# Seven-product blocks with turned signs: weight sums of a tile by accumulating DMA, sums of the second weights in one shared tile, and one borrowed weight slot

## The chip, the core and the metric

The kernel runs on one core of a Trainium2 chip. A core has TensorE (PE: matrix products; PEld is its weight load), VectorE (DVE), ScalarE (ACT), GpSimd (POOL) and SyncE (SP), which here only issues DMAs; sixteen DMA engines move data between HBM, the on-chip memory SBUF and back. Every engine works through its own list of instructions in order, and engines wait for each other through semaphores. Products land in PSUM, from where DVE and ACT take them. The metric is the device time of one launch in microseconds (us); less is better.

## The reference, cut to what matters

One step of a two-layer streaming encoder in float32: 1024 new frames and 64 sample frames, so 1088 columns of width 1024. Layer 0 is a Mamba-2 mixer, layer 1 is banded attention; each layer ends with the same feed-forward block, and the change touches only that block:

```python
def swiglu(u, w_in, w_out):
    g, up = jnp.split(u @ w_in, 2, axis=-1)
    return (jax.nn.silu(g) * up) @ w_out

xp = xp + rmsnorm(swiglu(rmsnorm(xp, nw[2]), ffn_w_in[layer], ffn_w_out[layer]), nw[3])
```

`w_in` is 1024 x 5632 (a gate half and an "up" half of 2816 = 22 tiles of 128 columns), `w_out` is 2816 x 1024.

## The kernel before, in words

**Precision.** A float32 operand is split into a high part in the 32-bit format that PE takes (`h`, made by a CAST on ACT, L354) and the rest (`lo`, a subtraction, L355, on DVE, or on POOL for one operand). A product is three matmuls: high x high, high x low, low x high (L1338, L1339, L1340).

**Seven products.** Weights and activations are cut in 2 x 2 blocks and multiplied with the seven products and fifteen sums of Strassen and Winograd. For pair `t` of weight tiles, `r0` is the gate tile, blocks b11 and b21, and `r1` is the up tile, blocks b12 and b22; each block is 128 x 512. The operands of the seven products (table `PRODS`) are `r0` (P1, P2), `ta` (P6, P7), `tb` (P5, P4) and `b22` (P3). Before, `Weights.pair` makes them so: POOL subtracts b22 - b12 (L302) and b12 - b11 (L303) into the tiles `tt`, DVE adds b11 (L320) and subtracts the result from b21 (L321), ACT and DVE split `r0`, `ta` and `tb` (three 128 x 1024 splits a pair), ACT and POOL split `b22` (128 x 512).

**Slots.** Split weights live in rings: `hl` of 3 slots (high and low, 1024 wide), `half` of 2 slots for `b22`, `raw` of 2 slots for what a DMA has just brought, `tt` of 2. A slot comes free after its last product: `W.put()` stands behind P2 (`r0`), P7 (`ta`), P4 (`tb`) and P3 (`half`) in the order P1, P6, P2, P7, P5, P4, P3.

**Stages of the feed-forward block,** in both layers. (1) Six pairs of tiles are multiplied plainly for the first column half (`plain_pairs`, lines "mmx"). (2) One pair, `t` = 6, is multiplied with seven products first for column block b = 0 (256 columns), then for b = 1 (288 columns); here called the first pair. (3) Fifteen pairs with both blocks in turn, so that a product's weights serve 544 columns: the shared pairs. (4) The six pairs of stage 1 again, for b = 1 alone, since b = 0 has them: the single pairs. A weight that serves 288 columns here costs the same splits. (5) The second weights `w_out`, seven products again (lines "po"), with the hidden activations read back from HBM (`hscr`).

**Gates.** The results of P1 to P7 are added up by DVE out of PSUM (L1353 to L1370, eight instructions of 288 or 256 columns a pair and block), with a SiLU on ACT (L1356, L1366) and two products on POOL (L1367 `u`, L1371 `c`). DVE then makes the sums of the hidden activations for stage 5 (L1469, L1477), which read `c` and `u` from POOL. In stage 3 DVE also makes the sums of the second weights (L1414), four instructions a job, 20 jobs a layer, with two tiles of their own (`r` 288 wide, `z` 272 wide); they are stored to HBM (`wsum`).

**What sets the order.** The kernel is recorded by a planner: `Stream` advances a clock by the columns that PE works through, side tasks come due on it, and a scheduler places the recorded instructions by priorities (`high_priority`) and dependencies, with a few ties given by hand (`add_manual_dep`, `behind`). PE's order is as written.

Of the kernel before, what the change touches and what calls it, by code (L numbers as in the profile page):

```python
# [43 lines left out]
RB_WAIT = 4.8  # L44
CHW = ((13.1, 8.8, 18.0), (7.5, 6.0, 20.5)), ((9.0, 5.2, 15.0), (10.5, 8.0, 21.0))
# [24 lines left out]
LENT = 3  # L70
SUM_P = 2.0
# [161 lines left out]

class Weights:
# [4 lines left out]
    def __init__(self, nc, raw, hl, half, tt):  # L239
        self.nc, self.raw, self.hl, self.half, self.tt = nc, raw, hl, half, tt  # L240
# [5 lines left out]
        self.raws, self.lent = [raw], None  # L246

        self.hx, self.used = Ring(None, "hx", 0, hl.shape, hl.dtype), []

    def plan(self, *items):  # L250
        for it in items:
# [3 lines left out]
            self.sq.append(it)  # L255

    def load(self):
# [4 lines left out]
        self.loaded = self.nc.sync.dma_start(r[:, :it.get("n", 1024)], it["src"][len(it["raw"])])  # L262
# [6 lines left out]
    def advance(self):  # L269
        moved = True  # L270
        while moved:
            moved = False
            while self.lq and any(r.free() for r in self.raws):
                self.load()
# [4 lines left out]
    def room(self):  # L279
        return self.hl.free() or self.hx.free()  # L280
# [13 lines left out]
    def pair(self, it):  # L294
        r0, r1 = it["raw"]
        b11, b21, b12, b22 = r0[:, :512], r0[:, 512:], r1[:, :512], r1[:, 512:]
        if "T" not in it:
            if not self.tt.free(2):
# [3 lines left out]
            g(ta[:, 512:], b22, b12, op=ALU.subtract)  # L302
            g(tb[:, :512], b12, b11, op=ALU.subtract)  # L303
            return True
        ta, tb = it["T"]
# [4 lines left out]
        if "r0" not in it:  # L310
            if not self.hl.free():
                return False
            self.part(it, "r0", self.hl, r0)
            self.ready.append(it)

            return False
        if "sums" not in it:
            v = self.nc.vector.tensor_tensor
            with self.tc.high_priority(self.pri):
                v(ta[:, :512], ta[:, 512:], b11, op=ALU.add)  # L320
                v(tb[:, 512:], b21, ta[:, :512], op=ALU.subtract)  # L321
            it["of"][0].put()
            it["sums"] = True
            return True
        for key, src in (("ta", ta), ("tb", tb)):
            if key not in it:
                if not self.hl.free():
# [1927 lines left out]
```

## Time and profile before

| | |
|---|---|
| median of 3 runs | 2914.21 us (2914.08 to 2914.99) |
| the profiled execution | 2919.82 us |
| its span, first to last instruction | 2918.0 us, so 1.8 us lie around it |
| mean granted TensorE clock | 0.995 |
| busy PE / DVE / ACT / POOL | 98% / 75% / 47% / 25% |
| layer 0, stages 2, 3, 4, 5 begin at | 917.8, 943.7, 1256.3, 1330.9 us |
| layer 1, the same | 2260.1, 2284.5, 2597.1, 2671.4 us |

The starts are those of the first matmul of a kind in the timeline. "Idle" in the profile's views is time before an instruction in which its engine did nothing, with the instruction that ended the wait behind an arrow. A view of windows gives each engine's busy time in a stretch, with the number of its instructions in brackets, the granted clock, the share of time that the 16 DMA engines were busy, and GB/s.

### The profile page before, as it was taken

To read this page: it belongs to the slowest core of one execution; us is meant where nothing else is said; L and a number is where in the kernel's file an instruction comes from. 1 tells how busy PE (TensorE), PEld (TensorE's weight loads), DVE (VectorE), ACT (ScalarE), POOL (GpSimd) and SP (SyncE) were. 2 spreads that over 40 slices of the span, in tenths; PEclk is the share of its full clock that TensorE was granted. 3 is DMA by queue.
4 is the path that set the end of the run, shared out by engine and by line. 5 is a ranking of instruction groups with operands and counts; after the bars stand their busy time and mean duration, and the time that the engine had idled before them with its cause. 6 is when DMAs were issued, how large, how long until landed. Compare 5 with 4: busy or idle time off the path is not lost. (4 is left out here: it accounts for less than half of the span.)

```text
span 2918.0 us, 58367 instructions
## 1 busy us (share of the span) xinstructions
PE 2852.8 (98%) x22094; PEld 2805.7 (96%) x22094; DVE 2191.3 (75%) x4994; ACT 1383.5 (47%) x2564; POOL 726.5 (25%) x900
## 2 busy tenths in 40 slices
PE   8999999999999999999998999999999999999999
PEld 8999999999999999999997899999999999999998
DVE  7987888885768667785569778777778876776567
ACT  6654546454444222244445556556565322334443
POOL 1333333331122343441021000000041334343011
PEclk9999999999999999999999999999999999999999
DMA  4423333244565556446564222222377455555656
GB/s 139 126 99 101 107 101 103 96 125 144 177 183 157 168 175 194 160 159 209 183 194 156 61 80 79 74 64 82 96 220 214 152 180 175 178 176 169 203 189 196
DMA packets 271530, 426.23 MB, mean 146 GB/s; under 512 B 25360, under 2 KB 202736, under 8 KB 271248
## 3 DMA queue, kind: packets, MB, share of 16 engines
q1 hardware_dynamic: 268016, 411.94, 44.4%
q0 software_dynamic: 3232, 10.56, 2.0%
q8 instruction: 174, 2.85, 0.4%
q14 instruction: 108, 0.88, 0.1%
HBM read 313.74 MB, written 104.19 MB: 143 GB/s over the span
## 5 line engine op out<-in xcount | busy, mean ns | idle before, releaser
L480 PE MATMUL mm<-r,hl 128*128 128x384 f32 (+2 forms) x1704 | 569.0, 334 | 6.1 <-DVE vt L1872 3.9
L481 PE MATMUL mm<-r,hl 128*128 128x384 f32 (+2 forms) x1704 | 551.4, 324 | 2.4 <-DVE r L1586 2.4
L482 PE MATMUL mm<-r,hl 128*128 128x384 f32 (+2 forms) x1704 | 551.1, 323 | 2.1 <-DMA hl<-in_w_in_dram 1.4
L1339 PE MATMUL px<-r,hl 128*128 128x288 f32 (+1 forms) x1184 | 348.1, 294 | 0.0
L480 PEld LDWEIGHTS mm<-r,hl 128*128 128x128 f32 x1704 | 323.4, 190 | 8.4 <-DVE vt L1872 4.2
L481 PEld LDWEIGHTS mm<-r,hl 128*128 128x128 f32 x1704 | 323.2, 190 | 3.3 <-DVE r L1586 3.0
L482 PEld LDWEIGHTS mm<-r,hl 128*128 128x128 f32 x1704 | 322.0, 189 | 2.8 <-DMA hl<-in_w_in_dram 1.7
L1340 PE MATMUL px<-r,hl 128*128 128x288 f32 x1056 | 312.7, 296 | 3.2 <-DVE hl L355 3.1
L1338 PE MATMUL px<-r,hl 128*128 128x288 f32 x1056 | 311.3, 295 | 2.8 <-DVE u L1353 2.1
L355 DVE TENSOR_TENSOR hl<-raw,hl 128x1024 fp32r<-128x1024 f32 (+2 forms) x172 | 193.7, 1127 | 99.1 <-ACT hl L354 98.8
L1712 PE MATMUL po<-r,hl 128*128 128x288 f32 (+1 forms) x856 | 246.9, 288 | 0.1
L1710 PE MATMUL po<-r,hl 128*128 128x288 f32 (+1 forms) x856 | 246.9, 288 | 0.0
L1711 PE MATMUL po<-r,hl 128*128 128x288 f32 (+1 forms) x856 | 246.9, 288 | 0.0
L1339 PEld LDWEIGHTS px<-r,hl 128*128 128x128 f32 x1184 | 223.0, 188 | 0.0
L354 ACT CAST hl<-raw 128x1024 fp32r<-128x1024 f32 (+2 forms) x172 | 166.5, 968 | 114.0 <-PE po L1712 34.3
L1340 PE MATMUL px<-rx,hl 128*128 128x256 f32 x768 | 215.0, 280 | 3.7 <-DVE hl L355 3.6
L1338 PE MATMUL px<-rx,hl 128*128 128x256 f32 x768 | 214.5, 279 | 1.5 <-ACT hl L354 1.5
L1340 PEld LDWEIGHTS px<-r,hl 128*128 128x128 f32 x1056 | 199.4, 189 | 4.6 <-DVE hl L355 4.6
L1338 PEld LDWEIGHTS px<-r,hl 128*128 128x128 f32 x1056 | 199.5, 189 | 3.7 <-DVE u L1353 2.5
L1339 PE MATMUL px<-rx,hl 128*128 128x256 f32 x640 | 178.9, 280 | 0.0
L1710 PEld LDWEIGHTS po<-r,hl 128*128 128x128 f32 x856 | 161.5, 189 | 0.0
L1712 PEld LDWEIGHTS po<-r,hl 128*128 128x128 f32 x856 | 160.9, 188 | 0.3 <-DVE hl L355 0.3
(385 smaller groups left out, 8152.2 us busy)
## 6 DMA issues: line engine op xcount, KB each, us to landing
raw<-in_w_f_dram SPq DMA_DIRECT2D x104, 512.0 KB, 4.2
raw<-in_w_in_dram SPq DMA_DIRECT2D x40, 512.0 KB, 3.9
MT<-ascr SPq DMA_DIRECT2D x48, 384.0 KB, 4.4
r<-hscr SPq DMA_DIRECT2D x58, 288.0 KB, 4.2
raw<-in_w_so_dram SPq DMA_DIRECT2D x32, 512.0 KB, 3.8
r<-in_w_f_dram SPq DMA_DIRECT2D x48, 288.0 KB, 3.4
wsum<-r SPq DMA_DIRECT2D x24, 576.0 KB, 3.4
r<-hscr SPq DMA_DIRECT2D x40, 256.0 KB, 4.2
```

The source lines that it names most:

```text
L354: self.nc.scalar.copy(h, v)
L355: (eng or self.eng or self.nc.vector).tensor_tensor(lo, v, h, op=ALU.subtract)
L480: PE.matmul(ps[:, :n], h_, xh, start=(first and i == 0), stop=False)
L481: PE.matmul(ps[:, :n], h_, xl, start=False, stop=False)
L482: PE.matmul(ps[:, :n], l_, xh, start=False, stop=(last and i == nk - 1))
L1338: PE.matmul(ps, wh, ah[:, k, :], start=(k == 0), stop=False)
L1339: PE.matmul(ps, wh, al[:, k, :], start=False, stop=False)
L1340: PE.matmul(ps, wl, ah[:, k, :], start=False, stop=(k == 3))
L1710: PE.matmul(ps, wh, xh, start=(k0 > 0 and i == ks[0]), stop=False)
L1711: PE.matmul(ps, wh, xl, start=False, stop=False)
L1712: PE.matmul(ps, wl, xh, start=False, stop=(k0 == 0 and i == ks[-1]))
```

## The change

Four things, all in the feed-forward block.

- **Signs turned, sums by DMA.** The four sums of a pair are taken with plus signs only; the activations' sums and the gates take the minus signs, one for one (a subtraction for an addition). SP loads b11 and b12 side by side into a tile of `tt` (a 2 x 512 pattern), and POOL issues an accumulating DMA that adds b12 and b22 to it from HBM: T = (b11 + b12, b12 + b22). DVE makes S = (T2 + b11, S1 + b21) into a tile of its own, `t2`. T and S are split as `ta` and `tb` were. `r1` is now only b22, and `b22` of every pair is split by two ACT instructions and an accumulating DMA on POOL, as four of the 44 were before. POOL's subtractions L302, L303 and L355 are gone. The first of two planner times, `ACC_W` = 5.0, stands between the load of T and its accumulation.
- **Products in another order:** P1, P6, P2, P7, P4, P5, P3; `s2` serves P6 and P4, `s1` P7 and P5. So `s2`'s slot comes free after P4 (the fifth product), `s1`'s after P5 (the sixth).
- **One job at a time for the sums of the second weights,** in one shared tile of the ring `R`, at any product whose gate result DVE has taken, with the planner time `SUM_W` = 4.5 from load to sums and from store to the next load. The tile pool `z` is gone, `t2` takes its place.
- **A borrowed slot:** in stage 4 (`HPC[0]` = 1; none in stage 5, `HPC[1]` = 0) a pair of tiles of the ring `RX` serves as a fourth slot beside `hl`.

```diff
+HPC = 1, 0
+class Pairs:          # two tiles of a ring, as high and low part of one slot
+    def free(self):
+        return self.live < self.cap and self.ring.free(2)
...
 class Weights:
     def advance(self):
         moved = True
         while moved:
             moved = False
+            while self.tq and self.tt.free():
+                it = self.tq.pop(0)
+                it["T"] = self.tt.get()
+                self.loaded = self.nc.sync.dma_start(it["T"].rearrange("p (e k) -> p e k", e=2), it["two"][0])
...
+                self.aq.append((self.clock() + ACC_W, it))
+            while self.aq and self.aq[0][0] <= self.clock() and 'two' in self.sq[0]:
+                it = self.aq.pop(0)[1]
+                x = self.nc.gpsimd.dma_start(it["T"], it["two"][1], accum_op=ALU.add)
...
     def pair(self, it):
         r0, r1 = it["raw"]
-            ta, tb = it["T"] = self.tt.get(), self.tt.get()
-            g = self.nc.gpsimd.tensor_tensor
-            g(ta[:, 512:], b22, b12, op=ALU.subtract)
-            g(tb[:, :512], b12, b11, op=ALU.subtract)
...
         if "b22" not in it and self.half.free():
-            self.part(it, "b22", self.half, b22, self.nc.gpsimd, it["pacc"] and it["src"][1][:, 512:])
+            self.part(it, "b22", self.half, r1[:, :512], None, it["src"][1])
...
-                v(ta[:, :512], ta[:, 512:], b11, op=ALU.add)
-                v(tb[:, 512:], b21, ta[:, :512], op=ALU.subtract)
+                x = v(S[:, :512], T[:, 512:], r0[:, :512], op=ALU.add)
+                v(S[:, 512:], S[:, :512], r0[:, 512:], op=ALU.add)
...
-        for key, src in (("ta", ta), ("tb", tb)):
+        for key, src, ring in (("s2", it["S"], self.t2), ("s1", it["T"], self.tt)):
...
-            ring = self.hl if ring or self.hl.free() else self.hx
+            ring = next(r for r in (self.hl, self.hx, self.hp) if r.free())
...
 PRODS = [
-    (P1, "r0", 0, 0), (P6, "ta", 0, 1), (P2, "r0", 512, 2), (P7, "ta", 512, 5),
-    (P5, "tb", 0, 3), (P4, "tb", 512, 6), (P3, "b22", 0, 4),
+    (P1, "r0", 0, 0), (P6, "s2", 0, 1), (P2, "r0", 512, 2), (P7, "s1", 512, 5),
+    (P4, "s2", 512, 6), (P5, "s1", 0, 3), (P3, "b22", 0, 4),
 ]
...
-            W.plan(dict(src=[w1[ORD[t_]], w1[FT + ORD[t_]]], pacc=t_ in (NB0, NB0 + 1)))
+            a, b = w1[ORD[t_]], w1[FT + ORD[t_]]
+            W.plan(dict(src=[a, b[:, 512:]], two=(w1[ORD[t_]:ORD[t_] + FT + 1:FT, :, :512].rearrange("e p k -> p e k"), b)))
...
+            def weight_sums(last):
+                if not job:
+                    if jobs and (part or R.free()) and len(ops[1].hl) == len(OPI):
...
+                        for e in range(2):
+                            src = w_f2[layer][2 * g + e].rearrange("p (h k) -> p h k", h=2)
+                            behind(nc.sync.dma_start(z[:, 2 * e:2 * e + 2, :], src[:, :, c:c + n]), W.loaded)
+                        job.append((st.t + SUM_W, g, c, n, z))
+                elif st.t >= job[0][0] and last is not None:
...
+                        for to, x, y in ((3, 3, 2), (2, 2, 0), (0, 3, 0), (1, 1, 0)):
+                            behind(V.tensor_tensor(z[:, to, :], z[:, x, :], z[:, y, :], op=ADD), last)
+                        nc.sync.dma_start(wsm_[layer][:, g, :, c:c + n], z)
...
-            if p_ in (P2, P7, P4, P3) and b == bs[-1]:
+            if p_ in (P2, P4, P5, P3) and b == bs[-1]:
                 W.put(p_ == P3)
...
-                        W.lent.cap = 2
+                        W.lent.cap, W.hp.cap = 2, HPC[0]
```

How the change moves instructions is shown at three places, in the scheduled lists of the two kernels. Line numbers of the changed kernel are its own: there L1388, L1390, L1394, L1397, L1400, L1401 and L1405 are the gate results of P6, P2, P7, P4, P5 (two) and P3; L351 and L353 are the two halves of S; L388 the split's subtraction; L1402 and L1406 POOL's products `u` and `c`; L1496 and L1504 the sums of hidden activations; L1447 a sum of second weights; L306 the accumulation into T, L381 that of b22. Numbers in names belong to the buffers.

**Single pairs (stage 4, layer 0), POOL.** One pair's work before, b22 - b12, `u`, the split of `b22`, b12 - b11, `c`:

```order
L302 TENSOR_TENSOR tt<-raw 128x512
L1367 TENSOR_TENSOR u_15602<-u_15602,c_15624 128x288
L355 TENSOR_TENSOR half<-raw,half 128x512
L303 TENSOR_TENSOR tt<-raw,rx 128x512
L1371 TENSOR_TENSOR c_15624<-p_15551,u_15566 128x288
```

and in the changed kernel:

```order
L1402 TENSOR_TENSOR u_15615<-u_15615,c_15630 128x288
L381 DMA half<-in_w_f_dram 128x512
L1406 TENSOR_TENSOR c_15630<-p_15562,u_15577 128x288
L306 DMA tt<-in_w_f_dram 128x1024
L1402 TENSOR_TENSOR u_15753<-u_15753,c_15768 128x288
```

Three instructions over 512 columns became two DMA issues; `c` no longer stands behind L355 and L303, but behind one issue.

**Single pairs, DVE,** about P6's and P2's gate results (`hl` is a split, `tt` and `t` the tiles T and S). Before:

```order
L355 TENSOR_TENSOR hl<-tt,hl 128x1024
L1370 TENSOR_TENSOR u_15566<-px,u_15566 128x288
L321 TENSOR_TENSOR tt<-rx,tt 128x512
L1353 TENSOR_TENSOR u_15700<-px,p_15685 128x288
L1477 TENSOR_TENSOR y_15568<-c_15624,y_15568 128x288
L1477 TENSOR_TENSOR c_15491<-c_15491,c_15624 128x288
L1477 TENSOR_TENSOR u_15602<-u_15602,y_15568 128x288
L1355 TENSOR_TENSOR p_15685<-px,p_15685 128x288
```

and in the changed kernel:

```order
L388 TENSOR_TENSOR hl<-raw,hl 128x1024
L1405 TENSOR_TENSOR u_15577<-px,u_15577 128x288
L351 TENSOR_TENSOR t_15680<-tt,raw 128x512
L353 TENSOR_TENSOR t_15680<-t_15680,raw 128x512
L1388 TENSOR_TENSOR u_15713<-px,p_15698 128x288
L1504 TENSOR_TENSOR y_15579<-y_15579,c_15630 128x288
L1504 TENSOR_TENSOR c_15495<-c_15495,c_15630 128x288
L1504 TENSOR_TENSOR u_15615<-u_15615,y_15579 128x288
L1390 TENSOR_TENSOR p_15698<-px,p_15698 128x288
```

Before, the second of the following pair's sums (L321) stands directly ahead of P6's result; now both halves of the following pair's S stand there. The three sums that read POOL's `c` keep their place between P6's and P2's results.

**First pair (stage 2, layer 0), DVE,** from the split of `r0` to that of `tb`; L1197 splits the activations of block b = 1. Before:

```order
L355 TENSOR_TENSOR hl<-raw,hl 128x1024
L1197 TENSOR_TENSOR r<-r 128x1152 x4
L355 TENSOR_TENSOR hl<-tt,hl 128x1024
L1469 TENSOR_TENSOR y_11115<-x 128x256
L1312 TENSOR_TENSOR x<-mmx,x 128x256
L320 TENSOR_TENSOR tt<-tt,raw 128x512
L1197 TENSOR_TENSOR r<-r 128x1152 x2
L1312 TENSOR_TENSOR x<-mmx,x 128x256
L1197 TENSOR_TENSOR r<-r 128x1152
L355 TENSOR_TENSOR hl<-tt,hl 128x1024
```

and in the changed kernel (there L1230 splits those activations, L1346 is a gate of the last plain pair), from S to the split of T:

```order
L351 TENSOR_TENSOR t_11144<-tt,raw 128x512
L1230 TENSOR_TENSOR r<-r 128x1152
L353 TENSOR_TENSOR t_11144<-t_11144,raw 128x512
L1230 TENSOR_TENSOR r<-r 128x1152
L1496 TENSOR_TENSOR y_11108<-x 128x256
L1230 TENSOR_TENSOR r<-r 128x1152
L388 TENSOR_TENSOR hl<-t_11144,hl 128x1024
L1346 TENSOR_TENSOR x<-mmx,x 128x256
L1230 TENSOR_TENSOR r<-r 128x1152
L1346 TENSOR_TENSOR x<-mmx,x 128x256
L1230 TENSOR_TENSOR r<-r 128x1152
L388 TENSOR_TENSOR hl<-tt,hl 128x1024
```

S now stands after the split of `r0` and between the activations' splits; before, both sums of this pair had been made by then, and a sum of the next pair (L320) stood ahead of the split of `tb`.

**Shared pairs (stage 3, layer 0), DVE,** from the last sum of one job of second weights to the first of the next in the changed kernel:

```order
L1447 TENSOR_TENSOR r<-r 128x256
L1405 TENSOR_TENSOR u_12061<-px,u_12061 128x288
L1388 TENSOR_TENSOR u_12302<-px,p_12270 128x256
L1388 TENSOR_TENSOR u_12317<-px,p_12285 128x288
L1504 TENSOR_TENSOR y_12063<-y_12063,u_12118 128x256
L1504 TENSOR_TENSOR u_12118<-u_11864,u_12118 128x256
L1504 TENSOR_TENSOR c_11894<-c_12148,y_12063 128x256
L1390 TENSOR_TENSOR p_12270<-px,p_12270 128x256
L1390 TENSOR_TENSOR p_12285<-px,p_12285 128x288
L1447 TENSOR_TENSOR r<-r 128x288
```

Both jobs use the same tile: between these two L1447 lie the store of the one and the load of the other on SP. Before, the two tiles took turns.

More of the change, by code (lines that the diff above doesn't have):

```diff
@@ L261, in load @@
         it["of"].append(ring)
-        self.loaded = self.nc.sync.dma_start(r[:, :it.get("n", 1024)], it["src"][len(it["raw"])])
+        src = it["src"][len(it["raw"])]
+        self.loaded = self.nc.sync.dma_start(r[:, :src.shape[1]], src)
         if self.behind is not None:
@@ L279, in room @@
     def room(self):
-        return self.hl.free() or self.hx.free()
+        return any(r.free() for r in (self.hl, self.hx, self.hp))
     def plain(self, it):
@@ L1395, in behind @@
                     tc.add_manual_dep(x.ins, last.ins.name, ORDER, reason="place in the order")
-            def load_sums(w):
-                n = w["n"]
-                if not jobs[n]:
-                    return
-                w["job"] = g, c = jobs[n].pop(0)
-                z = w["z"] = w["get"]()[:, :, :n]
-                for e in range(2):
-                    src = w_f2[layer][2 * g + e].rearrange("p (h k) -> p h k", h=2)
-                    behind(nc.sync.dma_start(z[:, 2 * e:2 * e + 2, :], src[:, :, c:c + n]), W.loaded)
@@ L1422, in hook @@
                         f[0](last)
-                elif p_ == P5 and len(ops[1].hl) == len(OPI):
-                    if len(workers) < 2 and R.free():
-                        r = R.get().rearrange("p (e n) -> p e n", e=4)
-                        workers.insert(0, dict(get=lambda: r, n=288))
-                    for w in workers:
-                        if "job" not in w:
-                            load_sums(w)
-                if (p_, t_ % 2) in ((P2, 0), (P7, 0), (P7, 1)):
-                    w = next((w for w in workers[::-1 if (p_, t_ % 2) == (P7, 0) else 1] if "job" in w), None)
-                    if w:
-                        sum_weights(w, last)
-            jobs = {288: [(g, 288 * c) for g in range(4) for c in range(3)], 272: [(g, 864 + 272 * c) for g in range(4) for c in range(2)]}
-            box, workers, due = [], [], []
+            box, due, job, part, done_ = [], [], [], [], [False]
+            jobs = [(g, c, min(288, HF * P - c)) for g in range(4) for c in range(0, HF * P, 288)]
             def hid_of(y, b, i, k=1):
@@ L1639, in back @@
                 W.behind = None
-                R.put(len(workers) - 1)
-                assert not any(jobs.values()) and not any("job" in w for w in workers) and len(summed) == 2 * HF
-            phase[0], W.lent.cap = 2, LENT
+                R.put(len(part))
+                assert not jobs and not job and len(summed) == 2 * HF
+            phase[0], W.lent.cap, W.hp.cap = 2, LENT, HPC[1]
             W.pri = WTP
```

125 lines of the change are left out of this document (74 added, 51 removed).

## The prediction

> **What bounds the kernel now.** First the page's busy times, then windows over the stages of the feed-forward block (first pair, shared, single, second weights of layer 0; first, single pairs of layer 1):
>
> ```profile
> span 2918.0 us, 58367 instructions
> PE 2852.8 (98%) x22094; PEld 2805.7 (96%) x22094; DVE 2191.3 (75%) x4994; ACT 1383.5 (47%) x2564; POOL 726.5 (25%) x900
> ...
> core 0: us, PE busy (x) PEld busy (x) DVE busy (x) ACT busy (x) POOL busy (x), PEclk, DMA share, GB/s
> 917.80:932.60 14.80, 11.90 (x86) 11.30 (x85) 13.08 (x20) 6.46 (x9) 3.70 (x4) 0.88 0.38 105
> 944.00:1256.30 312.30, 312.30 (x2520) 312.30 (x2519) 218.83 (x429) 94.54 (x158) 125.70 (x105) 1.00 0.56 179
> 1256.30:1330.90 74.60, 69.08 (x507) 66.97 (x506) 59.72 (x90) 29.07 (x47) 37.45 (x28) 1.00 0.45 141
> 1330.90:1550.00 219.10, 219.10 (x1771) 219.10 (x1770) 137.37 (x252) 99.07 (x181) 27.90 (x25) 1.00 0.62 197
> 2260.10:2273.50 13.40, 10.49 (x87) 9.90 (x86) 13.40 (x15) 8.24 (x11) 3.46 (x3) 1.00 0.31 79
> 2597.10:2671.40 74.30, 70.36 (x507) 68.48 (x505) 57.98 (x86) 27.68 (x44) 36.67 (x27) 0.98 0.43 139
> ```
>
> PE sets the time. In the shared pairs and in the second weights it never stops, so there the change can only lose. Time lies in the single pairs and the first pairs. What they would take without a stop follows from the spacing of matmuls:
>
> ```profile
> 1274.01 0.29 PE L1338 MATMUL px<-r,hl 128*128 128x288 f32 x1
> ...
> 1277.05 0.29 PE L1340 MATMUL px<-r,hl 128*128 128x288 f32 x1
> ```
>
> These are 24 matmuls in a row, 23 steps: 3.04 / 23 = 0.132 us for 288 columns. Six single pairs are 6 x 7 x 12 = 504 matmuls, 66.6 us; they take 74.6 and 74.3, so 8.0 + 7.7 = 15.7 us are lost. The shared window's mean step is 312.3 / 2520 = 0.124, so 256 columns take 2 x 0.124 - 0.132 = 0.116 us and a first pair's 84 matmuls for b = 0 take 9.7 us: 14.8 and 13.4 lose 5.1 + 3.7. In all 24.5 us can be had. PE's waits there:
>
> ```profile
> PE px L1340 <- DVE hl L355: 6.7, 7, 1.7
> ...
> PE px L1338 <- DVE p L1355: 4.0, 7, 0.9
> ...
> PE px L1338 <- DVE u L1353: 2.1, 2, 1.4
> ```
>
> It waits for DVE: for low parts of weights (L355), or for a PSUM bank that DVE has not emptied (L1353, L1355). Why DVE is late shows in one single pair (POOL, then DVE) and in the waits of that window:
>
> ```profile
> 1285.63 1.25 POOL L1367 TENSOR_TENSOR u<-u,c 128x288 f32<-128x288 f32 x1 [1.65 <-ACT u L1366]
> 1286.84 1.74 POOL L355 TENSOR_TENSOR half<-raw,half 128x512 fp32r<-128x512 f32 x1
> 1288.54 1.28 POOL L303 TENSOR_TENSOR tt<-raw,rx 128x512 f32<-128x512 f32 x1
> 1289.78 0.80 POOL L1371 TENSOR_TENSOR c<-p,u 128x288 f32<-128x288 f32 x1
> ...
> 1287.35 0.45 DVE L1353 TENSOR_TENSOR u<-px,p 128x288 f32<-128x288 f32 x1
> 1290.62 0.46 DVE L1477 TENSOR_TENSOR y<-c,y 128x288 f32<-128x288 f32 x1 [2.82 <-POOL c L1371]
> ...
> 1291.73 0.45 DVE L1355 TENSOR_TENSOR p<-px,p 128x288 f32<-128x288 f32 x1
> ...
> DVE y L1469 <- POOL c L1371: 5.3, 3, 2.8
> DVE y L1477 <- POOL c L1371: 4.4, 2, 2.8
> ```
>
> POOL's `c` stands behind 3.0 us of weight work; DVE, in order, stands 2.8 us for `c` with P2's result (L1355) behind it. That is 9.7 us of DVE in this window. With 59.7 us busy DVE is taken for 69.4 of 74.6 us, against PE's 66.6: DVE sets the single pairs' pace. And DVE's own work is stretched:
>
> ```profile
> L355 DVE TENSOR_TENSOR hl<-tt,hl x88: 1207/1220/2312, 918.3 to 2661.9; 128x1024 fp32r<-128x1024 f32 x88
> L320 DVE TENSOR_TENSOR tt<-tt,raw x40: 677/922/1787, 909.5 to 2652.1; 128x512 f32<-128x512 f32 x40
> L321 DVE TENSOR_TENSOR tt<-raw,tt x40: 674/964/1676, 911.5 to 2653.0; 128x512 f32<-128x512 f32 x40
> ```
>
> (minimum, median, maximum in ns.) The same instruction takes 0.67 us or 1.68, and what sets the two apart in the timeline is whether one of POOL's subtractions runs beside it.
>
> **The change part by part.** *POOL's subtractions go:* 44 each of L302 and L303 and 40 of L355. In their place stand 44 accumulations into T and 40 more into b22. The rows nearest to them:
>
> ```profile
> L350 POOL DMA_DIRECT2D hl<-in_w_f_dram x11: 844/859/874, 837.1 to 2246.3; - x11
> ...
> raw<-in_w_f_dram SPq DMA_DIRECT2D x104, 512.0 KB, 4.2
> ...
> hl<-in_w_f_dram POOLq DMA_DIRECT2D x11, 512.0 KB, 8.4
> ...
> half<-in_w_f_dram POOLq DMA_DIRECT2D x4, 256.0 KB, 4.7
> ```
>
> POOL then spends 2 x 0.86 = 1.7 us a pair where the pair above shows 1.74 + 1.28 and a L302. `c` stands behind one issue of 0.86 us instead of 3.0 us. It should be done before P6's result is taken: P3's result and `c` need 0.45 + 0.80 us, with the issue 2.1 us, and P1 and P6 last 2 x 12 x 0.132 = 3.2 us. So the wait of 9.7 us goes. Does the issue hold DVE up, as the subtractions did? Here they overlap:
>
> ```profile
> 920.97 0.86 POOL L350 DMA_DIRECT2D half<-in_w_f_dram  x1
> ...
> 921.06 0.69 DVE L320 TENSOR_TENSOR tt<-tt,raw 128x512 f32<-128x512 f32 x1 [0.86 <-POOL tt L302]
> ```
>
> 0.69 us is L320's short time, so I take no stretch.
>
> *DVE in a single pair, after:* three splits at 1.22, two halves of S at 0.69 (the row just above; up to 1.0 by the medians), eight gate results at 0.45, two activation sums at 0.45: 3.7 + 1.4 + 3.6 + 0.9 = 9.6 us, with the upper price 10.2, against PE's 11.1. DVE no longer sets the pace.
>
> *Slots.* With the new product order and three slots, `s2` would have three products (4.8 us) from P4's end to its use at P6 where `ta` had four. Among the shared pairs three products are 8.9 us, for a cast and a subtraction of 1.05 + 1.22 us: covered. For the single pairs the borrowed slot gives back more than that: `s2` takes `r0`'s slot five products before its use. So neither slots nor DVE stop PE there. I keep 2 us a layer for the entry (the second weights' activations are split there, 4 us of DVE ahead of `s1`) and the rest: 66.6 + 2 = 68.6, a gain of 6.0 + 5.7 = 11.7 us. Bounds: 0, if another wait takes the place (below), and the whole 15.7.
>
> *First pairs.* T needs load and accumulation, but is loaded as the last plain pair begins. The rows of layer 0 that this rests on, POOL's last accumulation before and DVE's splits of `ta` and `tb`:
>
> ```profile
> 904.38 0.84 POOL L350 DMA_DIRECT2D hl<-in_w_f_dram  x1 [5.16 <-PE mmx L482]
> ...
> 918.31 1.22 DVE L355 TENSOR_TENSOR hl<-tt,hl 128x1024 fp32r<-128x1024 f32 x1
> ...
> 925.81 1.22 DVE L355 TENSOR_TENSOR hl<-tt,hl 128x1024 fp32r<-128x1024 f32 x1
> ```
>
> One issue of 0.86 us after that and 8.4 us on, T is there at about 914, when DVE in its new order has just split `r0` (914.0, with 1.3 us for each activation split). S, its cast, its split with an activation split of 1.3 us between each: `s2` at 920.9, `s1` at 925.5, where the timeline has 919.5 for `ta` and 927.0 for `tb`. Then P6 loses 1.6 us and P7 1.8, 3.4 where 5.1 were lost: 1.7 us gained. By the same order layer 1 would lose 3.4 of now 3.7; I take 0.2. Bounds: 3 us either way in each, since an accumulation that lands at the longest, 10.9 us (quoted below), puts 2.5 us on both splits, and one that lands earlier lets the splits follow sooner.
>
> *ACT* gains a 512-wide instruction of 0.6 us in 40 pairs; it is busy 94.5 of 312.3 us, which hides it. *SP* gains a load a pair that waits for T's slot, with stores and `raw` loads queued behind it. A `raw` tile is asked for when S is made and split a pair later, 20.8 us (shared) or 11.1 us (single) for a load of 4.2 us; that room hides the wait for `s1`'s split, some 3 us. Without it the next split of `r0` would be late by as much.
>
> *DMA.* Prices by the queues' totals:
>
> ```profile
> q1 hardware_dynamic: 268016, 411.94, 44.4%
> q0 software_dynamic: 3232, 10.56, 2.0%
> ```
>
> 0.444 x 2918 / 411.94 = 3.1 us of all sixteen engines per MB, for accumulations 0.02 x 2918 / 10.56 = 5.5. A pair adds 0.26 MB of loads and 0.79 MB of accumulation: 5.2 us in the 20.8 us of a shared pair. The share there goes from 0.56 to 0.81. Under one, so nothing must stop, but landings get later.
>
> *Second weights' sums.* Same four sums, 20 jobs, but in one tile store, load and sums follow each other:
>
> ```profile
> DMA to landing us min/median/max: 3.1/3.5/6.1
> ...
> DMA to landing us min/median/max: 3.3/3.4/5.2
> ```
>
> (the loads L1406, the stores L1415.) Chain: 0.6 + 3.4 + 2 x 0.6 + 3.5 = 8.7 us. The tightest place in the new order leaves P3 to P2, three products, 8.9 us. Beyond it DVE stands with P7's results behind; PE stops one product (3 us) later. I take +1 us for all of it, bounds 0 and the second rival's.
>
> **Sum** against the profiled execution of 2919.8: -11.7 - 1.9 + 1 = -12.6, so 2907.2. That execution is 5.6 us above the median of the runs shown; on that scale 2901.6.
>
> **Rivals.** *The wait only moves.* In the single pairs DVE waits for T instead of `c`. Loop of a `tt` slot: load 4.2, accumulation 8.4, S 1.4, `s2` 1.05 + 1.22, `s1` 1.22 = 17.5 us, in two pairs' 22.2. It decides from 13 us of accumulation on; the longest of this kind is below:
>
> ```profile
> DMA to landing us min/median/max: 3.7/7.8/10.9
> ```
>
> At 15 us the loop gives 12 us a pair; the single pairs keep their 74 us: 2913. For it speaks the fuller DMA, against it the room. The Trainium skill, "DMA: Bandwidth & Descriptors", section "Anatomy of one DMA — SWDGE (gpsimd) path", fits 2.0 us + bytes / 436 per ns to a DMA from POOL, an estimate of 3.2 us for 512 KB; the loop would be 12.3 us and this rival dead. The trace's 7.8 contradicts it, for an accumulation, and is what I use.
>
> *Slower: the single tile stops PE.* If landings in the shared pairs stretch with the DMA share so that the chain of 8.7 passes 8.9 + 3 us, that is by 3.2 us over load and store together, DVE holds P7's results and PE stops. If 7 jobs of 20 in each layer are tight and lose 1.5 us: +21, in the sum -13.6 + 21 = +7, 2922. For it: the loads' longest, 6.1, at a share of 0.56. Against it: two landings must stretch at once, and most jobs have a wider gap. The Trainium skill, "DMA: Bandwidth & Descriptors", section "Issuing engines are not separate DMA queues", speaks for it: DMAs started by POOL and SP share the sixteen engines and interleave, so sums moved off POOL are not free. By that, latencies in the shared pairs rise; the trace before cannot show by how much.
>
> **How the numbers follow.** Forecast 0.68, with its own range 2892 to 2908 (all 24.5 us back would be 2890; half the single pairs' gain 2907). The moved wait 0.20 (2909 to 2917). Slower 0.12. That the change doesn't do what it says I leave out: in the new lists the accumulations, S and the splits into `rx` are there. The range 2892 to 2917 leaves out the slower case and a little below. Faster or slower counts from 0.2% (5.8 us), about what a measurement of this kernel can tell: faster 0.68, same 0.20, slower 0.12.
>
> **What would show it.** Right: single windows of 67 to 70 us, no wait of DVE for POOL's `c`, S at 0.7 us, the shared windows still 312 us at a DMA share near 0.8, a first pair of 13 us. Wrong: PE below its full busy time in the shared windows with DVE waiting for `r` (the single tile), DVE waiting for `tt` ahead of L351 in the single pairs (the moved wait), or single windows that stay at 74 us with DVE's splits late.

## The result, and the profile after

| | before | changed |
|---|---|---|
| median | 2914.6 us (2914.08 to 2919.0, 4 runs) | 2948.25 us (2944.86 to 2951.03, 4 runs) |
| ratio to before | | 1.0112 (95% interval 1.0094 to 1.0129) |
| first pair, block b = 0, layers 0 / 1 | 14.8 / 13.4 us | 16.7 / 16.6 us |
| shared pairs | 312.6 / 312.6 us | 327.9 / 325.7 us |
| single pairs | 74.7 / 74.4 us | 73.3 / 74.3 us |

The change makes the kernel 33.6 us slower; the prediction was 2901.6 us, with a range of 2892 to 2917. The stages are counted from first matmul to first matmul in the profiled runs. The shared pairs, for which the sum had a cost of 1 us, lose 15.3 + 13.1 us, and the single pairs, which were to gain 11.7 us, gain 1.5. The two profiled executions are 30.4 us apart in span, so what lies outside these stages differs by -1.6 us in sum.

The view of windows over the same stages of the changed kernel (first pair, shared, single of layer 0, then of layer 1) answers to the prediction's first fence:

```profile
span 2948.4 us, 58540 instructions
PE 2865.7 (97%) x22094; PEld 2818.0 (96%) x22094; DVE 2186.2 (74%) x4994; ACT 1408.9 (48%) x2604; POOL 577.4 (20%) x856
...
921.80:938.50 16.70, 12.82 (x87) 12.42 (x86) 13.45 (x20) 7.83 (x12) 1.59 (x3) 0.80 0.51 141
949.50:1277.40 327.90, 317.24 (x2522) 314.72 (x2521) 216.68 (x422) 101.44 (x172) 71.22 (x89) 0.99 0.77 217
1277.40:1350.70 73.30, 69.68 (x508) 69.45 (x507) 62.46 (x100) 36.19 (x58) 20.55 (x23) 0.95 0.82 221
2274.60:2291.20 16.60, 12.01 (x86) 11.45 (x85) 16.60 (x20) 10.67 (x12) 0.07 (x1) 0.90 0.21 45
2302.40:2628.10 325.70, 318.37 (x2522) 316.27 (x2522) 216.79 (x424) 101.57 (x172) 70.08 (x88) 0.99 0.79 223
2628.10:2702.40 74.30, 69.11 (x507) 68.41 (x507) 62.31 (x101) 36.45 (x59) 21.21 (x24) 0.98 0.82 219
```

In the shared pairs PE is no longer busy all the time, and the granted clock is 0.99 where it was 1.00. POOL's busy time there fell from 125.7 to 71.2 us, as the change meant, and the DMA share rose from 0.56 to 0.77 and 0.79.

**What stops PE there.** The waits of DVE and PE in the shared pairs of layer 0 (us in total, times, longest):

```profile
DVE r L1447 <- DMA r<-in_w_f_dram: 27.7, 8, 6.8
...
PE px L1372 <- DVE u L1394: 6.1, 5, 3.8
PE px L1372 <- DVE p L1390: 3.5, 2, 2.0
```

DVE waits for `r`, the tile of the second weights' sums, 8 times; layer 1 has 28.1 us of the same wait in 7. One such job, in the timelines of SP and DVE:

```profile
1211.88 0.39 SPq L1448 DMA_DIRECT2D wsum<-r  x1
1217.63 1.26 SPq L1441 DMA_DIRECT2D r<-in_w_f_dram  x2
...
1216.15 0.46 DVE L1390 TENSOR_TENSOR p<-px,p 128x288 f32<-128x288 f32 x1 [1.16 <-PE px L1374]
1223.43 0.95 DVE L1447 TENSOR_TENSOR r<-r 128x288 f32<-128x288 f32 x2 [6.82 <-DMA r<-in_w_f_dram]
1224.30 1.22 DVE L388 TENSOR_TENSOR hl<-raw,hl 128x1024 fp32r<-128x1024 f32 x1
1225.43 0.41 DVE L1394 TENSOR_TENSOR u<-u,px 128x256 f32<-128x256 f32 x1
```

The store goes at 1211.88, the load into the same tile 5.75 us later, when the store has landed, and DVE's sums at 1223.43, when the load has. P7's results (L1394) stand behind them, so that PE finds no free PSUM bank for its next product. Over all jobs the times from issue to landing, of the stores and then of the loads:

```profile
DMA to landing us min/median/max: 2.9/4.8/8.5
...
DMA to landing us min/median/max: 3.1/4.0/8.2
```

Between the 20 jobs of a layer lie 19 such chains, 38 in both. In 18 of them the first sum starts within 0.4 us of the load's landing (in 15 DVE stands idle for it). From the last sum of one job to the first of the next these 18 take 12.5 us (median), where the prediction had 8.7.

**A stop costs more than its length.** The first single pair of layer 0 (lines of PE, then windows around them):

```profile
1282.33 0.29 PE L1373 MATMUL px<-r,hl 128*128 128x288 f32 x1
1286.25 0.61 PE L1374 MATMUL px<-r,hl 128*128 128x288 f32 x1 [3.62 <-DVE hl L388]
...
1288.70:1291.70 3.00, 3.00 (x15) 3.00 (x14) 2.12 (x4) 0.41 (x1) 0.00 (x0) 0.50 1.01 339
1291.70:1296.00 4.30, 4.30 (x33) 4.30 (x33) 2.90 (x5) 3.49 (x5) 1.68 (x2) 0.98 0.85 242
```

After the stop of 3.62 us the granted clock is 0.50 until 1291.7: 23 steps of mostly 0.24 us instead of 0.132 take 2.6 us more. For all stops, let the length be the time from one matmul's start to the next, less the usual step. Of ten stops of 2.0 us or more in the seven-product stages of the changed kernel, seven are followed, at once or up to ten matmuls later, by 13 to 26 matmuls at half pace; of the ten shorter ones (0.7 us or more) none has more than five.

### The profile page after: what moved, and what is told of

It reads as the page before. It is cut to its first block, busy times and chain, and to the rows that moved or that the text cites. A ratio compares the mean times of both kernels' runs of the same rounds, so it can differ in the third digit from the quotient of the medians.

```text
span 2948.4 us, 58540 instructions
## 1 busy us (share of the span) xinstructions
PE 2865.7 (97%) x22094; PEld 2818.0 (96%) x22094; DVE 2186.2 (74%) x4994; ACT 1408.9 (48%) x2604; POOL 577.4 (20%) x856
## 5 line engine op out<-in xcount | busy, mean ns | idle before, releaser
L1373 PE MATMUL px<-r,hl 128*128 128x288 f32 (+1 forms) x1120 | 331.6, 296 | 0.0
L514 PEld LDWEIGHTS mm<-r,hl 128*128 128x128 f32 x1704 | 322.7, 189 | 3.4 <-DVE r L1613 3.1
L1374 PE MATMUL px<-r,hl 128*128 128x288 f32 x992 | 295.8, 298 | 8.0 <-DVE hl L388 8.0
L1372 PE MATMUL px<-r,hl 128*128 128x288 f32 x992 | 295.3, 298 | 4.6 <-DVE p L1390 3.0
L388 DVE TENSOR_TENSOR hl<-raw,hl 128x1024 fp32r<-128x1024 f32 (+2 forms) x166 | 189.8, 1144 | 98.3 <-ACT hl L387 98.2
L1373 PEld LDWEIGHTS px<-r,hl 128*128 128x128 f32 x1120 | 213.5, 191 | 0.0
L1374 PEld LDWEIGHTS px<-r,hl 128*128 128x128 f32 x992 | 189.7, 191 | 8.7 <-DVE hl L388 8.7
L1372 PEld LDWEIGHTS px<-r,hl 128*128 128x128 f32 x992 | 189.6, 191 | 6.4 <-DVE p L1390 4.1
L1736 PEld LDWEIGHTS po<-r,hl 128*128 128x128 f32 x860 | 162.3, 189 | 0.0
L1372 PEld LDWEIGHTS px<-rx,hl 128*128 128x128 f32 x768 | 147.4, 192 | 15.4 <-DVE u L1394 9.8
```

The lines of the kernel that those rows point to most:

```text
L388: self.low = (eng or self.eng or self.nc.vector).tensor_tensor(lo, v, h, op=ALU.subtract)
L514: PE.matmul(ps[:, :n], h_, xl, start=False, stop=False)
L1372: PE.matmul(ps, wh, ah[:, k, :], start=(k == 0), stop=False)
L1373: PE.matmul(ps, wh, al[:, k, :], start=False, stop=False)
L1374: PE.matmul(ps, wl, ah[:, k, :], start=False, stop=(k == 3))
L1736: PE.matmul(ps, wh, xh, start=(k0 > 0 and i == ks[0]), stop=False)
```

## The experiments

All times are medians; ratios are to the kernel before on the same chip, with 95% intervals.

### Is it the single tile, or the fuller DMA?

Three kernels that differ from the changed kernel (e1, e2) or from the kernel before (e3) in the second weights' sums alone.

```diff
 e1  -  for to, x, y in ((3, 3, 2), (2, 2, 0), (0, 3, 0), (1, 1, 0)):   # changed kernel, DVE's sums left out
     -      behind(V.tensor_tensor(z[:, to, :], z[:, x, :], z[:, y, :], op=ADD), last)
 e2  +  with tc.high_priority(HIP):        # changed kernel, around the four sums and their store
 e3  the kernel before, with weight_sums() of the changed kernel; the tile z and the workers are gone
```

> The changed kernel without the four DVE sums of a job of second weights (L1447); the loads into the shared tile and the stores from it stay, so the DMA work is the same, and the stored sums are not the reference's. Theory A, the single tile: DVE's waits for r (27.7 and 28.1 us in the shared pairs) are gone and the shared windows go from 331 and 327 us back to 312 to 316; the whole 2948 - 19 - 18 = 2911, between 2906 and 2917. Theory B, the fuller DMA slows the shared pairs through other waits: the windows stay above 322 us each and the whole above 2932.

> The changed kernel with the four sums of a job and their store recorded at high priority, so that they stand together behind one product's gate result: in the scheduled list the last sum of a job and the first of the next are then never under 4 products apart (11.9 us), where 10 of 38 places have 3 (8.9 us) in the changed kernel. Theory A with a chain of 11.5 us: most of the waits of DVE for r go, from 28 us a layer to below 10, and the shared pairs lose 5 to 8 us a layer instead of 18; the whole 2920 to 2930. Theory B: no change, 2943 to 2950.

> The kernel before with the changed kernel's way of summing the second weights: one job at a time in one tile of R, the tile z gone, the same gaps in DVE's list (3 products at 11 of 38 places). POOL's subtractions and the DMA share of 0.56 in the shared pairs stay. If the single tile alone is enough: DVE waits for r 20 us or more a layer and the whole is 2935 to 2950. If it takes the single tile and the fuller DMA together: chain 8.7 us against 8.9, waits under 6 us a layer, the whole 2914 to 2921. Theory B (only the DMA): 2914 to 2916.

| | time | ratio | shared pairs, layers 0 / 1 |
|---|---|---|---|
| e1 | 2925.94 us | 1.0025 (1.0013 to 1.0038) | 316.8 / 317.6 us |
| e2 | 2927.91 us | 1.0030 (1.0017 to 1.0042) | 316.6 / 322.5 us |
| e3 | 2982.92 us | 1.0216 (1.0192 to 1.0240) | 342.9 / 343.2 us |

e3 decides: the kernel before, with its old subtractions on POOL and its old traffic, loses 30 us a layer by the changed kernel's way with these sums (a lone tile, one job at a time, the four sums at low priority). Its windows and a wait of the first:

```profile
944.00:1286.90 342.90, 322.61 (x2522) 316.89 (x2522) 226.90 (x425) 89.47 (x157) 121.33 (x104) 0.99 0.51 162
2314.20:2657.40 343.20, 325.08 (x2522) 320.89 (x2521) 231.40 (x432) 91.10 (x158) 121.27 (x104) 0.98 0.51 165
...
DVE r L1415 <- DMA r<-in_w_f_dram: 26.4, 7, 5.6
```

At a DMA share of 0.51, 16 of 38 chains end on the load, with a median of 11.6 us. So the tile is enough without the fuller DMA: these 11.6 us are, by the medians of their parts, 4.1 for the store, 1.9 for the load's place in SP's list, 0.6 between its two halves and 4.6 for its landing. e3 was expected at 2935 to 2950 if the tile alone is enough. It took more, and its shared pairs lose about twice what the changed kernel's lose. In its layer 0 DVE also waits 27.9 us for POOL's b22 - b12 (11.4 in the kernel before), but how the two waits make up the loss was not tested.

e2 gives the sums of a job one place: in the changed kernel they were spread over up to three products by their low priority, which left 3 products (8.9 us) to the next job at 10 of 38 places; with 4 at least, 11.3 us come back in layer 0 and 3.2 in layer 1, where one load that lands after 9.3 us keeps DVE standing for 7.1 us.

e1 was expected at 2906 to 2917 and missed it: the expectation took the shared pairs' loss for 19 + 18 us (by the first matmuls it is 15.3 + 13.1), and 4 to 5 us a layer stay. Without the sums SP's store waits for the load itself, some 5 us a job, with the stores of `c` behind it, for which DVE waits 10.2 us in layer 0.

f4 (below) sets the jobs 5 products apart. Its shared pairs of both layers:

```profile
940.90:1253.50 312.60, 312.60 (x2522) 312.60 (x2521) 209.68 (x411) 101.90 (x168) 74.51 (x89) 1.00 0.77 217
2297.30:2610.80 313.50, 313.10 (x2523) 312.66 (x2522) 211.25 (x415) 100.97 (x168) 74.21 (x89) 1.00 0.79 220
```

With 18 of a layer's 20 jobs (two slip into the single pairs) and the same DMA share of 0.77 and 0.79, layer 0 takes the kernel before's own 312.6 us and layer 1 only 0.9 more. So the fuller DMA by itself does not slow the shared pairs. The whole does not gain by it: f4's single pairs take 89.6 and 88.6 us. No run has the sums by DMA with two tiles for the second weights, so what that part of the change is worth alone stays open.

### What the borrowed slot and POOL's relief are worth

```diff
 e4  -HPC = 1, 0                            # changed kernel without the slot
     +HPC = 0, 0
 g3  +HPC = 1, 0                            # kernel before: class Pairs, a third ring in part() and room()
     +    W.lent.cap, W.hp.cap = 2, HPC[0]
 h1  -    pacc=t_ in (NB0, NB0 + 1)         # g3, with b22 of the single pairs by accumulating DMA
     +    pacc=t_ <= NB0 + 1
```

> The changed kernel without the borrowed slot (HPC = 0, 0). If the shorter single pairs (69.6 and 70.5 us against 74.6 and 74.3) come from POOL's relief, they stay within 1 us and the whole stays at 2946 to 2951. If they come from the slot, s2 waits for room and the single windows go back to 74 us: the whole 2955 to 2960.

> The kernel before with the borrowed slot alone (HPC = 1, 0), POOL's subtractions and two tiles for the second weights kept. Taking the slot from the changed kernel cost 6 us in each layer's single pairs. If the slot itself brings that, the single pairs here fall from 74.7 and 74.4 to 69 to 70 us and the whole to 2906 to 2910. If DVE's wait for POOL sets the single pairs before (the prediction's reading), they stay at 73 to 75 and the whole at 2914 to 2918.

> The kernel before with the borrowed slot (g3, 2909.7) and with b22 of the single pairs split by ACT and an accumulating DMA instead of POOL. It takes 1.74 us a pair off POOL ahead of its product c, and adds 0.26 MB of accumulation a pair. If POOL's place still costs the single pairs of g3 (70.9 and 71.7 us against 66.6 without a stop), they fall to 68 to 70 and the whole by 2 to 6 us to 2904 to 2908. If the slot was the whole gain: single pairs within 1 us of g3's, the whole within 2 us. If accumulations cost the single pairs: 73 us or more.

| | time | ratio | single pairs, layers 0 / 1 |
|---|---|---|---|
| e4 | 2960.00 us | 1.0140 (1.0115 to 1.0166) | 79.5 / 80.4 us |
| g3 | 2909.66 us | 0.9965 (0.9947 to 0.9983) | 70.9 / 71.7 us |
| h1 | 2906.32 us | 0.9956 (0.9943 to 0.9970) | 69.2 / 70.5 us |

```profile
1254.00:1324.90 70.90, 68.45 (x508) 67.19 (x507) 60.21 (x88) 27.32 (x44) 35.76 (x28) 1.00 0.49 149
2589.90:2661.60 71.70, 68.28 (x507) 67.06 (x507) 59.64 (x88) 27.17 (x44) 36.04 (x28) 1.00 0.46 147
...
1253.60:1322.80 69.20, 67.70 (x508) 67.00 (x507) 59.18 (x89) 30.80 (x51) 33.19 (x28) 1.00 0.60 175
2586.10:2656.60 70.50, 68.27 (x508) 67.09 (x507) 58.42 (x88) 31.16 (x50) 32.78 (x28) 1.00 0.59 170
```

(g3, then h1.) The slot carries the single pairs: 6 us a layer in the changed kernel, 3.8 and 2.7 us when it is put alone on the kernel before, whose POOL still does all its subtractions and lets DVE wait 6.7 us a layer for `c` (9.7 and 9.3 before). By its single pairs g3 falls between the two cases of its expectation: neither "the slot is all" (69 to 70 us) nor "POOL sets the pace" (73 to 75). Taking b22 off POOL adds 1.7 and 1.2 us a layer by the windows; the two totals overlap in their intervals, so that part rests on the windows alone. Both kernels are faster than the two that were compared, h1 by 0.44% of the kernel before.

### What stops the first pairs and the single pairs of the changed kernel

```diff
 f1  e2, and   +  if "cast" in it and self.pri == HIP:      # first pair: cast of b22 behind that of r0
               +      self.tc.add_manual_dep(x.ins, it["cast"].ins.name, ORDER, ...)
 f2  e2, and   -  if t_ == FT - 1: ... st.spawn(loader())   # loader of hidden activations one pair later
               +  elif t_ == 0 and phase[0]: st.spawn(loader())
 f3  f1 and f2
 f4  f3, and   +  SUM_W, STORE_W = 5.6, 5.4                 # jobs 5 products apart, also behind P1
 g1  f4 without f2
 g2  g1, and   +  yield 0, 2.0, lambda: room(b, k)          # between two groups of the loader
 h2  f1, with the loader behind the last single pair
 i1  f1, with b22 of the single pairs split by POOL again
```

> The kernel with the early sums (2927.9), and in the first pair the cast of b22 ordered behind the cast of r0 on ACT. Theory: in the first pair ACT stood 8.4 us for b22's raw tile with the casts of the activations of b = 1 behind it, and DVE 6.2 us for those; b22 is needed only by the last product. Then the first pairs go from 16.3 and 15.6 us to 11.5 to 13 us (P1 and P6 lose under 1 us each) and the whole to 2919 to 2923. If instead T's accumulation is what lands late, the first pairs stay at 15 to 16.5 us and the whole at 2925 to 2930.

> The kernel with the early sums, and the loader of the hidden activations started one single pair later, so that its seven splits into rx no longer stand in DVE's list ahead of the first single pair's split of s1. Theory: the entry costs 3.9 and 5.3 us (products 1, 2 of the first single pair) and goes; single pairs 68 to 70 us instead of 71.8 and 75.1, the whole 2917 to 2922. If the work only moves, another product of the single pairs stops for it: single pairs within 1.5 us of before the edit, the whole 2925 to 2930.

> Early sums, b22's cast later, loader later. If the three stops are separate, the gains add: 2927.9 - 7 - 8 = 2913, between 2909 and 2917, which is the time of the kernel before. If they share a cause, 2918 to 2924.

> As f3, and the jobs of second weights set apart: SUM_W 5.6 from load to sums, 5.4 from store to load, and P1's place allowed, so that 5 products (14.8 us) lie between two jobs at all but 2 places a layer, where f3 has 4 (11.9 us) at half of them. Theory A, chain of 11.5 us, up to 15 with a late load: DVE's waits for r go from 18.9 us to under 5, the stop of 7 us in layer 1 (a load landing after 9 us) goes; the whole 5 to 8 us below f3. If the remaining waits for r are hidden, it equals f3 within 2 us.

> As f4 (early sums, jobs set 5 products apart, b22's cast later in the first pair), but the loader at its old time. In f4 the shared pairs took 312.6 and 313.5 us, the kernel before's own time at the fuller DMA share; the single pairs took 89.6 and 88.6. If the loader's later start made the single pairs long: 73 to 77 us a layer here, and the whole 2945.7 - 2 x 14 = 2918, between 2914 and 2922. If the two jobs of second weights that slip into the single pairs made them long: they stay above 82 us and the whole above 2932.

> As g1, with 2 us between two groups of the loader in the single pairs, so that its splits into rx stand one to three at a time in DVE's list instead of seven in a row ahead of s1's split. If the row of splits is what stops the first single pair (5.0 + 1.3 us in layer 0, 5.0 + 0.3 in layer 1), the single pairs fall to 68 to 71 us and the whole 8 to 10 us below g1. If the loads of hidden activations are late because the DMA engines are full at the entry, the stop moves on as in f2: single pairs at or above g1's.

> As f1 (changed kernel, early sums, b22's cast later), with the loader of the hidden activations started only behind the last single pair, so that no load, cast or split of it lies in the single pairs; the second weights then wait for it, which is not what is looked at. If the loader is what stops the single pairs (6.3 us at the entry in layer 0, 5.4 in layer 1): windows of 66.6 to 69 us, the prediction's 68.6. If accumulations that land late stop them: 71 us or more.

> As f1 (changed kernel, early sums, b22's cast later), with b22 of the six single pairs split by POOL again, so that of two accumulations a single pair only T's stays: 0.26 MB of accumulation a pair less, and 1.7 us of POOL a pair more. If the fuller DMA (share 0.84) makes T late, T's load and accumulation land earlier and the single pairs fall from 73.6 and 72.7 to 70 to 71 us. If T's own chain (slot, load, accumulation, sums, split) is too long whatever else moves: 72 to 75 us. If POOL ahead of c decides: 76 us or more.

| | time, us | ratio | first pairs, us | shared | single |
|---|---|---|---|---|---|
| e2 | 2927.91 | 1.0030 | 16.3 / 15.6 | 316.6 / 322.5 | 71.8 / 75.1 |
| f1 | 2927.58 | 1.0038 (1.0025 to 1.0052) | 14.6 / 15.4 | 316.5 / 322.4 | 73.6 / 72.7 |
| f2 | 2943.69 | 1.0092 (1.0078 to 1.0105) | 14.4 / 15.2 | 314.0 / 326.8 | 81.3 / 79.7 |
| f3 | 2938.01 | 1.0078 (1.0066 to 1.0091) | 14.9 / 15.9 | 313.7 / 320.1 | 81.1 / 80.9 |
| f4 | 2945.65 | 1.0097 (1.0082 to 1.0113) | 14.7 / 15.1 | 312.6 / 313.5 | 89.6 / 88.6 |
| g1 | 2934.05 | 1.0049 (1.0030 to 1.0068) | 13.9 / 14.1 | 312.6 / 316.7 | 79.6 / 84.4 |
| g2 | 2934.91 | 1.0050 (1.0030 to 1.0069) | 14.9 / 15.3 | 312.6 / 315.0 | 82.3 / 81.4 |
| h2 | 2964.68 | 1.0156 (1.0138 to 1.0175) | 12.7 / 13.9 | 313.2 / 322.7 | 76.8 / 77.2 |
| i1 | 2930.38 | 1.0042 (1.0028 to 1.0056) | 12.6 / 15.8 | 313.8 / 322.1 | 76.4 / 76.2 |

(Two numbers are layers 0 and 1. h2's single pairs are counted to the end of their last product, since the loader stands behind it.) f2, f3 and f4 came out slower than both cases of their expectations: by single pairs of about 80 us in f2 and f3, and of 89 in f4.

*First pair.* In the changed kernel ACT stands for b22's raw tile, and DVE for ACT:

```profile
915.37 0.62 ACT L379 CAST half<-raw 128x512 fp32r<-128x512 f32 x1 [8.35 <-DMA raw<-in_w_f_dram]
...
917.08 1.36 DVE L1230 TENSOR_TENSOR r<-r 128x1152 fp32r<-128x1152 f32 x1 [6.17 <-ACT r L1229]
```

f1 puts `r0`'s cast ahead of this one and was expected to give 2.6 to 4.8 us a layer; it gives 1.7 and 0.2, as much as the same stage moves between kernels that do not differ in it (16.3 in e2, 14.4 in f2; 14.6 in f1, 12.6 in i1). The total did not move. What DVE waits for in f1's layer 0:

```profile
911.45 0.69 DVE L351 TENSOR_TENSOR t<-tt,raw 128x512 f32<-128x512 f32 x1 [4.12 <-DMA tt<-in_w_f_dram]
```

That is T (3.7 us in layer 1), the other case of f1's expectation. In the changed kernel T's load landed 7.6 us after its issue in layer 0, the accumulation behind it 7.9 us after its own at 911.40, so T was there at 919.3, 1.8 us before S. Both operands were late, and with one wait out of the way the other shows.

*Entry to the single pairs.* DVE's list in the changed kernel, with the loader's splits (L1533) ahead of that of `s1` (L388):

```profile
1281.81 3.25 DVE L1533 TENSOR_TENSOR rx<-rx 128x512 fp32r<-128x512 f32 x5
1284.98 1.21 DVE L388 TENSOR_TENSOR hl<-tt,hl 128x1024 fp32r<-128x1024 f32 x1
```

P7's product stops for that split. Of the 6.7 us that layer 0's single pairs take above 66.6, this stop and the half clock behind it are 6.3 (5.0 in the product where it falls and 1.3 in the next). From there on PE hardly stops in this layer. In layer 1 the entry takes 5.3 us, and two later products lose 1.0 us each, one behind a wait for T:

```profile
2663.75 0.69 DVE L351 TENSOR_TENSOR t<-tt,raw 128x512 f32<-128x512 f32 x1 [3.96 <-DMA tt<-in_w_f_dram]
...
2665.59 0.40 PE L1372 MATMUL px<-r,hl 128*128 128x288 f32 x1 [0.83 <-DVE u L1388]
```

With the loader one pair later (f2) P7 of the first single pair loses nothing in either layer, so the loader's place is the cause of the entry's stop. But it cannot simply be moved. Later (f2) or behind the stage (h2), other products stop instead, and the stage takes longer; spread (g2), it takes longer than in g1 in one layer and less in the other. In h2, with no loader, the stop is here (POOL, ACT, DVE in turn):

```profile
1277.58 0.88 POOL L306 DMA_DIRECT2D tt<-in_w_f_dram  x1 [5.65 <-DMA tt<-in_w_f_dram]
...
1283.22 1.04 ACT L389 CAST rx<-tt 128x1024 fp32r<-128x1024 f32 x1 [7.54 <-DMA tt<-in_w_f_dram]
...
1284.30 1.23 DVE L390 TENSOR_TENSOR rx<-tt,rx 128x1024 fp32r<-128x1024 f32 x1 [8.19 <-ACT rx L389]
1285.44 1.22 DVE L390 TENSOR_TENSOR hl<-tt,hl 128x1024 fp32r<-128x1024 f32 x1
1286.58 0.45 DVE L1402 TENSOR_TENSOR u<-px,u 128x288 f32<-128x288 f32 x1
```

T's load keeps POOL 5.65 us, the accumulation lands 5.6 us after its issue, ACT stands 7.5 us for T, DVE 8.2 us for ACT, and P5's result (L1402) and PE behind them. i1 was to tell whether T is late because the engines are full. It does not: its single pairs, 76.4 and 76.2 us, fall into the case of POOL, and the stop that grew is the entry's. DVE in i1, then POOL:

```profile
1259.17 4.32 DVE L1536 TENSOR_TENSOR rx<-rx 128x512 fp32r<-128x512 f32 x5
...
1260.50 1.74 POOL L390 TENSOR_TENSOR half<-raw,half 128x512 fp32r<-128x512 f32 x1
```

The five splits take 4.32 us beside POOL's subtraction, where they took 3.25 without one; the stop behind them goes from 5.0 to 6.1 us. That agrees with the loader's place as the cause of the entry's stop, and shows DVE stretched beside POOL's subtraction. What makes T late in h2 (full engines, or the length of its own chain) stays open; a third tile for T was not tried. Why g1's single pairs take 79.6 and 84.4 us stays open too: two jobs of second weights slip into them there, beside the loader, and neither half of its expectation fits both layers.

## Why the prediction was wrong

**Second weights' sums, "+1 us": the step that failed.** The shared pairs lost 28.4 us; without the sums 9.2 of it stay (e1), with the jobs set apart 0.9 (f4). The chain was worked out from medians of idle times, 3.4 + 3.5 us of landing, and set against the place in the order, 8.9 us. In the jobs that count it is 12.5 us (store 5.6, load 4.9, issues and SP's list the rest), and even with the old traffic 11.6 (e3). The rival "the single tile stops PE", given 0.12, was the right mechanism: where it had 7 of 20 jobs a layer, DVE waits at 8 and 7, and its price of 21 us measured 28.4. What was said against it, that two landings must stretch at once, did not hold it off. At the jobs that count they did stretch, by 2.2 + 1.4 = 3.6 us where the rival asked for 3.2. And so much is not needed: at a share of 0.51 e3 has the stops with 0.7 + 1.1 us more of landing and 1.9 us of SP's list. The chain left out SP's list, and the price of a stop left out the half clock behind it. The sentence that in the shared pairs the change "can only lose" was right and should have set the chances: a chain of 8.7 us in a room of 8.9, with a longest landing of 6.1 us in the rows already quoted, is no term of 1 us.

**Single pairs, "-11.7 us":** 1.5 us. The forecast that PE hardly stops beyond the entry is what the trace of layer 0 shows. "I keep 2 us a layer for the entry" is the failed term: it takes 6.3 us in layer 0 and 5.3 in layer 1. The cause of the old loss was half right. DVE's wait for POOL's `c` does go (no row of it is left in the single pairs of either layer), but "so neither slots nor DVE stop PE there" hid that the slot was the larger part: 6 us of a layer hang on it (e4), and alone on the kernel before it gives 3.8 and 2.7 (g3), b22's relief 1.7 and 1.2 more (h1).

**First pairs, "-1.9 us":** +5.1 us. The bound of 3 us either way held for layer 0 (+1.9) and not for layer 1 (+3.2). The step that failed is "T is there at about 914": it counts one accumulation behind POOL's last one and leaves out T's own load, and in layer 0 T was there at 919.3. ACT's 8.35 us for b22's raw tile was not in the sum either. In layer 0 it held S up to 921.1, after T; without it DVE waits for T (f1). How the loss divides between the two is not shown.

**The rival "the wait only moves"** (DVE waits for T) shows once in the changed kernel's single pairs at a price: 4.0 us of DVE in layer 1, 1.0 us of PE. h2 shows it in full: once the loader is out of the way, T stops the single pairs at 77 us, above its 74.

**What was right:** S at its short time,

```profile
L351 DVE TENSOR_TENSOR t<-tt,raw 128x512 f32<-128x512 f32 x40 | 28.4, 711 | 5.3 <-DMA tt<-in_w_f_dram 5.3
L353 DVE TENSOR_TENSOR t<-t,raw 128x512 f32<-128x512 f32 x40 | 28.1, 703 | 0.7
```

with medians of 0.68 and 0.69 us (means 0.71 and 0.70) where the sums before had medians of 0.92 and 0.96; a DMA share near 0.8 in the shared pairs (0.77, 0.79) that by itself costs nothing (f4); and the sign to look for, PE below its full busy time with DVE waiting for `r`. The stores' median landing went from 3.4 to 4.8 us at the fuller share. The Trainium skill, "DMA: Bandwidth & Descriptors", section "Issuing engines are not separate DMA queues", by which such DMAs interleave on the same engines, agrees with that row; e3 adds that the stops do not need it.

## What to carry to other kernels

Two tiles that are worked in turn hide a store and a load behind each other; made one, they form a chain, and a chain belongs beside the tightest gap between two uses in the scheduled order, with the longest landings, the issuing queue's list and the engine's own list behind it, before any gain is counted. Where one edit of several is doubtful, price the edits apart: here one borrowed slot on the old kernel is worth 0.35%, and the package that held it cost 1.1%. A stop that is moved by moving the work in front of it has to be looked for again at the next operand in line.

## What was not expected of the hardware

In the changed kernel's seven-product stages a stop of PE of 2 us or more is in seven cases of ten followed by 3.2 to 5.7 us at half the granted clock, so that it costs 1.5 to 2.7 us beyond its length (13 to 26 steps of 0.24 us for one of 0.132; 2.6 us after the stop of 3.62 above). The Trainium skill, "TensorE: Matmul & The Clock Gate", section "What's actually happening", has the array at half rate after an idle window of about 3.4 us and until as long a busy one; the trace agrees on the half rate and, in five of the seven, on its length (3.2 to 3.3 us; 5.7 in the other two), and shows it after shorter stops too, of 1.35 us once in the kernel before and 2.15 us in the changed one, while a stop of 2.2 us elsewhere had none.

The four sums of a job, recorded together at low priority, were spread over up to three products in DVE's list, which brought their store later and the next job's gap down to 3 products; recorded at high priority they stand in one place, and the whole goes from 1.0112 to 1.0030 of the kernel before (e2).
